# Differential heads' probabilities turned in 32x32 blocks and carried through DRAM, with values eight steps later

## The chip, the cores and the metric

The kernel runs on one core of a Trainium2 chip. The metric is the device time of one execution in microseconds (us), from three runs. The core has TensorE (matrix products, into PSUM), VectorE, ScalarE and GpSimd, and DMA queues issued from SyncE (SP) and GpSimd. In the profile these are PE (and PEld for its weight loads), DVE, ACT, POOL and SP.

## The reference

One transformer layer on 512 rows of width 1024, all in float32: half a SwiGLU feed-forward, a token mixer, half a second SwiGLU feed-forward, and a final RMS norm. The change lies in the mixer. It has four differential heads (numbers 0 to 3 in the kernel) and eight dilated heads, which the kernel handles in pairs as units 4 to 7. Both are called heads below. A differential head has two score maps, m = 0 and 1:

```python
s = einsum('bhmqd,bhmkd->bhmqk', q_blk, k) * scale
s = where(dist >= 0, s + bias, -inf)
p = softmax(s, axis=-1)
a = p[:, :, 0] - lam * p[:, :, 1]
out = einsum('bhqk,bhkd->bhqd', a, v)        # then a norm over the head's 128 columns
```

The map is causal, so with 512 rows in four blocks of 128 the rows of block i have i + 1 blocks of keys: 128, 256, 384 and 512 columns, 1280 in all. The heads' outputs, side by side, are multiplied by `w_out`.

## The kernel before, in words

Products that need more precision than one pass are made of three: both operands are split into a rounded high part and the remainder (names ending in h and l, `mh` and `ml` among them), and `mm3` (L187 to L190) issues high-high, high-low and low-high. ScalarE makes the high parts, VectorE the remainders.

The mixer is one list of TensorE chunks, the projections of queries, keys and values for all heads, and from step 92 the output projection. `step(t)` (L2042) issues chunk t. `put(t, rank, f)` hangs other work on a step: rank under 10 goes before the chunk, in order of rank, and from 10 behind it. The order on TensorE is the order written. The other engines' order is made by the tile framework, which also sets the waits; it gives a tile's buffer to the next tile of the same tag only when everything that reads or writes the old tile is done. Tags `pr0` and `pr1`, the probabilities of map 0 and 1, have two buffers each, and so have the score banks `s` and the banks `t` in PSUM.

A projection chunk is six 512-column matmuls, a head's projection is eight chunks. Head u starts its scores at step s = 41, 49, 57, 65, 73, 81, 88 and 97 for u = 0 to 7.

- Keys and queries (L1596 to L1692). When the projection is done, `casts_k` casts the upper half of the bank (map 0's 64 rows) into k0 and the lower half into k1; `evac_k` has VectorE make the remainders l0 and l1 from the halves (L1645) and has SP copy each half of each tile into its other half (`other_half`, L1639), so that the query's two parts, one above the other, meet the same keys. `casts_q` and `rests_q` do the queries.
- Scores (`score`, L1730): two matmuls for each block of rows i and map m, then VectorE adds the bias, takes the extremum (mx) and writes the row into `pr0` or `pr1`; ScalarE takes the exponential in place. Two steps are given to each block of rows.
- `combine` (L1745): VectorE scales map 1's rows and adds them to map 0's, so `pr0` holds the head's one matrix.
- `turn` (L1869): TensorE transposes the ten 128x128 blocks of that matrix (L1879), at steps s+9 and s+11 (one step apart for head 0), into `t` banks; ScalarE copies them to a tile with tag `tx` (L1881).
- `values` (L1884), step s+13: ten products, two instructions each, of a turned block and a block of values (L1891).
- `squares`, `mean`, `scale`, `finish`, `finish_low` (steps s+14, s+15, s+18, s+20, s+21): the norm. GpSimd takes the power, VectorE scales the output of all four blocks at once out of PSUM (L1915), TensorE transposes it (L1921), ScalarE writes `mh[u]`, VectorE `ml[u]`.

Heads 5 and, in part, 6 already go another way. `flip` (L1761) has VectorE turn 32x32 blocks of 128x640 (L1766), `away` sends the result to a DRAM tile in four DMAs, one for each 32 partitions, in runs of 1280 bytes (L1772), and `back` reads it in one (L1783) so that the blocks themselves are turned too. Their products are `values_moved` (L1797). Head 6's other half is turned by TensorE in `turn_rows` (L1785), head 4 and head 7 by `turn_part`. Heads 4 to 7 share one `tx` tile, made by `turned_tx`.

SP issues in one queue, in the framework's order: weights (L1401), bias strips (L1165), the key copies (L1640), and the DMAs of `away` and `back`.

The output projection (L2020 to L2024) runs over slices k = 0 to 7, one for each head's `mh` and `ml`, and over four blocks of rows; a chunk has two slices of one block of rows.

Of the kernel before, what the change touches and what calls it, by code (L numbers as in the profile page):

```python
# [14 lines left out]
F32 = mybir.dt.float32  # L15
# [3 lines left out]
ALU = mybir.AluOpType  # L19
# [18 lines left out]
DIRECT = (7,)  # L38
MOVED = {5: (0, 1), 6: (1,)}
PAIRED_ROWS = 5  # L40
BACK = {5: 7, 6: 9}
TAKEN = {5: 16, 6: 13}
# [85 lines left out]
def tile_macaron(ctx: ExitStack, tc, xs, xT, wf, wgu1, wst1, wdg1, wqk, wvd, wo, wgu2, wst2,  # L128
# [1055 lines left out]
    def cast(o, a):  # L1184
        A.copy(o, a)

    def rest(o, a, h):
        V.tensor_tensor(o, a, h.bitcast(F32), op=ALU.subtract)
# [407 lines left out]
    def qk_chunks(u):  # L1596
# [26 lines left out]
        def casts_k():  # L1623
            _, _, k0, k1, _, _ = qk[u]
            pk = st["pk"]
            cast(k0[lo, :], pk[lo, :])
            cast(k1[hi, :], pk[hi, :])

# [6 lines left out]
        def evac_k():  # L1635
            q0, q1, k0, k1, l0, l1 = qk[u]
            pk = st["pk"]

            def other_half(t, a, b):  # L1639
                nc.sync.dma_start(t[b, :].bitcast(F32), t[a, :].bitcast(F32))  # L1640

            other_half(k0, lo, hi)
            other_half(k1, hi, lo)
            for a, b, kx, lx in ((lo, hi, k0, l0), (hi, lo, k1, l1)):
                rest(lx[a, :], pk[a, :], kx[a, :])  # L1645
                other_half(lx, a, b)

# [62 lines left out]
    def attention(u, s):  # L1710
        diff, quick, moved = u < 4, u == 7, u in MOVED
        st = {}
        order = (1, 2, 0, 3) if u >= PAIRED_ROWS else range(NQ)

        def row(m, i):
            w = (i + 1) * P
            if u < PAIRED_ROWS:
                return st["pr"][m][:, OFF[i]:OFF[i] + w]
            o = m * 640 + (0, 0, 2 * P, P)[i]
            return st["pr"][i in (1, 2)][:, o:o + w]  # L1720
# [64 lines left out]
        def turn_rows(part):  # L1785

            tx = st["x", 0] = turned_tx()[:, :1280]
            pt = pp.tile([P, S], F32, tag="t", name=f"pt{u}{part[0][0]}{part[0][1]}", bufs=2)
            n = 0
            for m, i in part:  # L1790
                o = m * 640 + (0 if i == 0 else P)
                for k in range(i + 1):
                    T.transpose(pt[:, n + k * P:n + (k + 1) * P], row(m, i)[:, k * P:(k + 1) * P], ident[:])
                A.copy(tx[:, o:o + (i + 1) * P], pt[:, n:n + (i + 1) * P])
                n += (i + 1) * P

        def values_moved():  # L1797
# [20 lines left out]
        def turn_part(m, part):  # L1818
# [9 lines left out]
            if "tx" not in st:  # L1828
                st["tx"] = turned_tx()
                st["used"] = 0  # L1830
            if quick:
# [14 lines left out]
                return  # L1846
            ptb = st["tx"][:, st["used"]:st["used"] + n]
            st["used"] += n
            A.copy(ptb[:, :n], pt[:, :n])
# [19 lines left out]
        def turn(tiles):  # L1869

            if "tx" not in st:
                st["tx"] = tp.tile([P, 12 * HS], F32, tag="tx", name=f"ptx{u}", bufs=1)
            for own in tiles:
# [38 lines left out]
        def scale():  # L1912
            po3, ob = st["po3"], st["ob"]
            V.tensor_tensor(st["f2"], st["f2"], st["y"][:], op=ALU.mult)
            V.tensor_tensor(ob, po3, st["f"][:].to_broadcast([P, NQ, P]), op=ALU.mult)  # L1915

# [33 lines left out]
        if diff:  # L1950

            step, tv = 2 if u else 1, s + 13
            put(tv - 2 - step, 2, turn, ((0, 2), (1,)))
            put(tv - 2, 2, turn, ((3,),))
            put(tv, 1, values)
            e = tv + 1
            put(e, 7, squares)
            put(e + 1, 7, mean)
            put(e + 4, 7, scale)
            put(e + 6, 3, finish)  # L1960
            put(e + 7, 8, finish_low)
        elif quick:
# [8 lines left out]
        elif moved:  # L1971
# [14 lines left out]
        else:  # L1986
            tv = s + 9
            parts = ((0, 0, 4),), ((1, 1, 4),), ((2, 2, 4), (3, 3, 4))
            for j, part in enumerate(parts):
                for m in range(2):  # L1990
                    put(tv + j, 2, turn_part, m, part)
                put(tv + 4, 1, values_part, part)
            put(tv + 5, 3, finish)
            put(tv + 5, 8, finish_low)

# [307 lines left out]
```

## Time and profile before

| | |
|---|---|
| Three runs | 906.12, 906.31, 906.56 us; median 906.31 |
| The profiled execution | 906.15 us, of which 904.4 are its span, from the first to the last instruction |
| Granted TensorE clock, mean | 0.999 |
| ScalarE copies of turned blocks (L1881) | 12 |
| Key copies by SP (L1640) | 28 DMAs of 128 KB |
| DMA in the whole span | 153.05 MB, mean 169 GB/s |

Rows of the profile have the engine, the line of the kernel, the operation, the tile written and the tiles read, the shape (partitions x elements) and a count. In the views in order of time the first two columns are the start in us from the span's start and the length; a bracket at the end has the idle time of the engine ahead of the instruction and what ended it. In the view of one line the three numbers are the shortest, median and longest length in ns. For DMAs the time to landing is that from issue to the last byte's arrival. A row of a DMA queue has the packets, the megabytes and the time of its packets as a share of 16 engines over the window.

### The profile page before, as it was taken

Reading aid. Unit: us, or ns where it says so; the run is one execution under the profiler, and the core shown is the slowest. Engines: PE = TensorE matmul, PEld = TensorE weight load, DVE = VectorE, ACT = ScalarE, POOL = GpSimd, SP = SyncE. Lnnn points to the kernel's source line nnn. Section 1 sums busy time; section 2 is a strip of 40 time slices with the busy share of each in tenths; the row PEclk is TensorE's granted clock in tenths of the full one; section 3 lists DMA queues with packets and bytes.
Section 4 is the critical chain, followed back from the end, with each engine's and each line's share of the span. In section 5 each row is a group of like instructions: output and inputs, shape, how many; then the busy total and the mean of one; then the engine's idle time right before and its main releaser. Section 6 shows DMA issues by size and latency. Waiting matters only on the chain.

```text
span 904.4 us, 15918 instructions
## 1 busy us (share of the span) xinstructions
PE 894.2 (99%) x5640; PEld 803.6 (89%) x5640; DVE 752.0 (83%) x1519; ACT 566.2 (63%) x1192; POOL 118.3 (13%) x148
## 2 busy tenths in 40 slices
PE   9999999999999999999999999999999999999997
PEld 7888998899998889888888768989999889999885
DVE  7698998889888888887887945888888888988985
ACT  7355666466667766757777665656666546666573
POOL 0101202121122110100000000111112112212200
PEclk9999999999999999999999999999999999999999
DMA  7464869677789663624443713475779679779902
GB/s 259 128 164 121 237 180 241 151 198 185 193 220 276 181 194 84 154 89 141 117 134 99 233 59 117 95 185 138 186 180 247 162 178 247 199 188 237 267 13 93
DMA packets 73903, 153.05 MB, mean 169 GB/s; under 512 B 8480, under 2 KB 10528, under 8 KB 73824
## 3 DMA queue, kind: packets, MB, share of 16 engines
q1 hardware_dynamic: 56240, 119.84, 41.2%
q0 software_dynamic: 17584, 32.20, 21.9%
q8 instruction: 44, 0.72, 0.3%
q14 instruction: 35, 0.29, 0.1%
HBM read 144.24 MB, written 4.10 MB: 164 GB/s over the span
## 4 chain that ended last, share of the span: by engine, by line
PE 94%; DVE 2%; DMA 1%; ACT 1%; issue 1%; SPq 0%; POOLq 0%; DVEq 0%; ACTq 0%
PE pt L188 8%; PE pt L189 8%; PE pt L190 8%; PE pua L188 2%; PE pua L190 2%; PE pua L189 2%; PE pq L188 2%; PE pq L189 1%; PE pk L190 1%; PE pq L190 1%; PE pk L189 1%; PE pk L188 1%; PE pwo L190 1%; PE pwo L188 1%; PE pwo L189 1%; PE pga L188 1%
## 5 line engine op out<-in xcount | busy, mean ns | idle before, releaser
L1742 ACT ACTIVATE pr<-pr,mx 128x128 f32<-128x128 f32 (+3 forms) x64 | 35.9, 562 | 28.4 <-DVE mx L1739 27.3
L544 DVE SCALAR_TENSOR_TENSOR x<-pt,x 128x512 f32<-128x512 f32 x50 | 33.2, 687 | 19.8 <-PE pt L190 12.6
L1739 DVE CUSTOM_DVE_ANT_0 pr<-sc,strip 128x128 f32<-128x128 f32 (+3 forms) x64 | 30.6, 486 | 6.8 <-PE sc L1737 6.0
L450 DVE TENSOR_TENSOR w<-s2b,w 128x512 fp32r<-128x512 f32 x38 | 26.0, 685 | 8.0 <-ACT w L446 8.0
L446 ACT CAST w<-raa 128x512 fp32r<-128x512 f32 x34 | 20.9, 622 | 18.6 <-DVE raa L414 10.3
L446 ACT CAST w<-s2b 128x512 fp32r<-128x512 f32 x38 | 23.6, 620 | 6.3 <-DVE s2b L419 6.3
L446 ACT CAST w<-rab 128x512 fp32r<-128x512 f32 x28 | 17.1, 622 | 16.3 <-DVE rab L414 7.5
L188 PE MATMUL pwo<-w,mh 128*128 128x512 f32 x64 | 25.9, 405 | 0.2 <-ACT mh L1929 0.2
L190 PE MATMUL pwo<-w,ml 128*128 128x512 f32 x64 | 25.1, 393 | 0.5 <-DVE ml L1938 0.5
L189 PE MATMUL pwo<-w,mh 128*128 128x512 f32 x64 | 25.0, 390 | 0.0
L450 DVE TENSOR_TENSOR w<-s2a,w 128x512 fp32r<-128x512 f32 x30 | 20.5, 684 | 3.0 <-ACT w L446 2.8
L446 ACT CAST w<-s2a 128x512 fp32r<-128x512 f32 x30 | 18.6, 621 | 6.6 <-DVE s2a L419 5.8
L1736 PE MATMUL sc<-k,q 128*128 128x128 f32 (+3 forms) x64 | 21.9, 343 | 0.8 <-DVE mx L1739 0.8
L450 DVE TENSOR_TENSOR w<-raa,w 128x512 fp32r<-128x512 f32 x34 | 22.6, 683 | 0.0
L189 PE MATMUL pxgb<-ttb,w 128*128 128x256 f32 x80 | 22.5, 281 | 0.0
L221 POOL TENSOR_TENSOR fin<-fin,half 128x1 f32<-128x1 f32 (+1 forms) x7 | 4.0, 568 | 137.3 <-DVE fin L1286 85.7
L389 POOL DMA_DIRECT2D s1bg<-wst_dram x10 | 8.7, 873 | 92.8 <-DVE w L450 38.8
L1737 PE MATMUL sc<-l,q 128*128 128x128 f32 (+3 forms) x64 | 20.4, 320 | 0.0
L189 PE MATMUL pxub<-ttb,w 128*128 128x256 f32 x72 | 20.2, 281 | 0.0
L389 POOL DMA_DIRECT2D s1ag<-wst_dram x8 | 7.1, 888 | 94.8 <-DMA s1ag<-wst_dram 32.9
L1416 DVE TENSOR_TENSOR w<-raw_qk,w 128x512 fp32r<-128x512 f32 x24 | 16.5, 688 | 3.6 <-ACT w L1412 3.5
L221 POOL TENSOR_TENSOR yi<-ss,half 128x4 f32<-128x4 f32 x4 | 4.1, 1015 | 113.0 <-DVE ss L1908 113.0
(1176 smaller groups left out, 3932.2 us busy)
## 6 DMA issues: line engine op xcount, KB each, us to landing
raw_qk<-wqk_dram SPq DMA_DIRECT2D x12, 512.0 KB, 3.5
raw0bg<-wst_dram SPq DMA_DIRECT2D x10, 512.0 KB, 5.4
raw0bu<-wst_dram SPq DMA_DIRECT2D x9, 512.0 KB, 5.7
raw_gua<-wgu_dram SPq DMA_DIRECT2D x8, 512.0 KB, 3.6
raw0ag<-wst_dram SPq DMA_DIRECT2D x8, 512.0 KB, 4.9
strip<-bias_rows SPq DMA_DIRECT2D x16, 256.0 KB, 3.7
raw_wo<-wo_dram SPq DMA_DIRECT2D x8, 512.0 KB, 3.5
raw0au<-wst_dram SPq DMA_DIRECT2D x7, 512.0 KB, 5.9
```

Of the source, the lines that this page charges most:

```text
L188: T.matmul(po, wh, mh, start=first, stop=False, skip_group_check=on)
L189: T.matmul(po, wh, ml, start=False, stop=False, skip_group_check=on)
L190: T.matmul(po, wl, mh, start=False, stop=last, skip_group_check=on)
L389: nc.gpsimd.dma_start(t[:], b, accum_op=ALU.add)
L446: A.copy(made[t][0], source(t))
L450: V.tensor_tensor(l, source(t), h.bitcast(F32), op=ALU.subtract)
L544: V.scalar_tensor_tensor(o, a, f, b, op0=ALU.mult, op1=op1)
L1416: V.tensor_tensor(l[:, c:c + 512], raw[:, c:c + 512], h[:, c:c + 512].bitcast(F32), op=ALU.subtract)
L1736: T.matmul(ps[:, :w], qs[:, qi], ks[:, :w], start=True, stop=False)
L1737: T.matmul(ps[:, :w], qs[:, qi], ls[:, :w], start=False, stop=True)
L1739: V.tensor_tensor_reduce(out=pi, in0=ps[:, :w], in1=st["b"][m][:, w - 1::-1], op0=ALU.add, op1=ALU.min, scale=1.0, scalar=3.0e38, accum_ou ...
L1742: A.activation(pi, pi, AF.Exp, scale=-1.0, bias=st["mx"][:, m, i:i + 1], accum_out=st["ls"][:, m, i:i + 1])
```

## The change

For heads 0 to 3:

- `turn` and `values` are replaced by `diff_flip`, `diff_away`, `diff_back` and `diff_values`. The rows are scored in the order 1, 2, 0, 3 and lie in `pr0` so that rows 1 and 2 fill columns 0 to 639 (group n = 1) and rows 0 and 3 columns 640 to 1279 (group 0). VectorE turns the 32x32 blocks of each group into `pr1` of the same head, whose rows are no longer needed, at step s+8 (group 1) and s+12 (group 0). SP sends each group to a DRAM tile in four DMAs, whose runs in DRAM are 32 floats, and reads it at s+13 and s+17 in one DMA, with runs of 640 floats, into one half of the shared `tx` tile, which heads now use in turn. The products follow at s+21, eight steps later than before, and everything behind them moves with them (head 3's `finish` and `finish_low` by one step less).
- `scale` multiplies by ScalarE, block of rows by block of rows, in place of one VectorE operation, and one step earlier in relation to the products.

For the keys of heads 0 to 6: one cast of all 128 rows into k1 and one remainder into l1, in place of two half ones each. k1 and l1 then hold map 0's keys above map 1's, and SP copies: the upper half into both halves of k0 (and l0), then the lower half over k1's (and l1's) upper half. That is six DMAs in place of four, the last two of which overwrite what the first ones read.

Also: head 4's turning and products come one or two steps later, at fixed places in the shared tile; head 5's first `back` one step later; head 6's `turn_rows` takes the two short rows first and copies them in one operation; the output projection's three chunks of slices 4 and 5 take slice 4 for three blocks of rows first, then slice 5.

```diff
+MOVED_DIFF = (0, 1, 2, 3)
+DIFF_FLIP = (12, 8)
+DIFF_BACK = (17, 13)
+DIFF_TAKEN = 21
+PART_PLACES = {(0, 0): 0, (1, 0): 2560, (0, 1): 512, (1, 1): 896, (0, 2): 1280, (1, 2): 1664}
-BACK = {5: 7, 6: 9}
+BACK = {5: 8, 6: 9}
...
         def casts_k():
-            cast(k0[lo, :], pk[lo, :])
-            cast(k1[hi, :], pk[hi, :])
+            cast(k1[:], pk[:])
...
-            def other_half(t, a, b):
-                nc.sync.dma_start(t[b, :].bitcast(F32), t[a, :].bitcast(F32))
-
-            other_half(k0, lo, hi)
-            other_half(k1, hi, lo)
-            for a, b, kx, lx in ((lo, hi, k0, l0), (hi, lo, k1, l1)):
-                rest(lx[a, :], pk[a, :], kx[a, :])
-                other_half(lx, a, b)
+            rest(l1[:], pk[:], k1[:])
+            for t0, t1 in ((k0, k1), (l0, l1)):
+                for b in (lo, hi):
+                    nc.sync.dma_start(t0[b, :].bitcast(F32), t1[lo, :].bitcast(F32))
+            for t in (k1, l1):
+                nc.sync.dma_start(t[lo, :].bitcast(F32), t[hi, :].bitcast(F32))
...
+            if u in MOVED_DIFF:
+                o = (5 * P, 0, 2 * P, 6 * P)[i]
+                return st["pr"][m][:, o:o + w]
...
+        def diff_flip(n):
+            o = (1 - n) * 640
+            t = st["tr", n] = st["pr"][1][:, o:o + 640]
+            V.transpose(t.rearrange("p (c b j) -> p b c j", c=4, b=5), st["pr"][0][:, o:o + 640])
+
+        def diff_away(n):
+            st["pd", n] = d = dp.tile([32, 20, 4, 32], F32, tag=f"pe{n}", name=f"pe{u}{n}")
+            for r in range(4):
+                nc.sync.dma_start(d[:, :, r, :], st["tr", n][32 * r:32 * r + 32, :].rearrange("p (x a) -> p x a", a=32))
+
+        def diff_back(n):
+            o = u % 2 * 1280 + n * 640
+            st["x", n] = turned_tx()[:, o:o + 640]
+            nc.sync.dma_start(st["x", n], st["pd", n][:].rearrange("j (c b) r a -> c j (b r a)", c=4))
+
+        def diff_values():
+            st["po"] = mm_bank(f"po{u}")
+            st["po3"] = st["po"][:].rearrange("p (i d) -> p i d", i=NQ)
+            fo = (u % 4) * P
+            for i, n, b in ((1, 1, 0), (2, 1, 2), (0, 0, 0), (3, 0, 1)):
+                for k in range(i + 1):
+                    T.matmul(st["po3"][:, i, :], st["x", n][:, (b + k) * P:(b + k + 1) * P], vt[0, k][:, fo:fo + P],
+                             start=k == 0, stop=k == i)
...
-                A.copy(tx[:, o:o + (i + 1) * P], pt[:, n:n + (i + 1) * P])
                 n += (i + 1) * P
+            if len(part) > 1:
+                A.copy(tx.rearrange("p (m e) -> p m e", m=2)[:, :, :P], pt[:, :n].rearrange("p (m q) -> p m q", m=2))
+            else:
+                A.copy(tx[:, o:o + n], pt[:, :n])
...
         def scale():
-            V.tensor_tensor(ob, po3, st["f"][:].to_broadcast([P, NQ, P]), op=ALU.mult)
+            for i in range(NQ):
+                A.activation(ob[:, i, :], po3[:, i, :], AF.Copy, scale=st["f2"][:, i:i + 1])
...
-            step, tv = 2 if u else 1, s + 13
-            put(tv - 2 - step, 2, turn, ((0, 2), (1,)))
-            put(tv - 2, 2, turn, ((3,),))
-            put(tv, 1, values)
+            step, tv = 2 if u else 1, s + (DIFF_TAKEN if u in MOVED_DIFF else 13)
+            if u in MOVED_DIFF:
+                for n in range(2):
+                    put(s + DIFF_FLIP[n], 9.2, diff_flip, n)
+                    put(s + DIFF_FLIP[n], 9.3, diff_away, n)
+                    put(s + DIFF_BACK[n], 2, diff_back, n)
+                put(tv, 1, diff_values)
...
-            put(e + 4, 7, scale)
-            put(e + 6, 3, finish)
-            put(e + 7, 8, finish_low)
+            put(e + 3, 5, scale)
+            put(e + 6 - (u == 3), 3, finish)
+            put(e + 7 - (u == 3), 8 if u < 3 else 1, finish_low)
...
-                for n, part in enumerate((((0, 3),), ((1, 3),), ((0, 0), (1, 0)))):
+                for n, part in enumerate((((0, 0), (1, 0)), ((0, 3),), ((1, 3),))):
...
-        chunks += [lambda kp=kp, tt=tt: wo_mm(0, tt, (2 * kp, 2 * kp + 1)) for tt in range(3)]
+        chunks += [lambda kp=kp, tt=tt: wo_mm(0, tt, (2 * kp, 2 * kp + 1)) for tt in range(3)] if kp < 2 else [
+        lambda part=part: [wo_mm(0, tt, (k,)) for k, tt in part]
+        for part in (((4, 0), (4, 1)), ((4, 2), (5, 0)), ((5, 1), (5, 2)))]
```

More of the change, by code (lines that the diff above doesn't have):

```diff
@@ L1712, in attention @@
         st = {}
-        order = (1, 2, 0, 3) if u >= PAIRED_ROWS else range(NQ)
+        order = (1, 2, 0, 3) if u >= PAIRED_ROWS or u in MOVED_DIFF else range(NQ)
         def row(m, i):
             w = (i + 1) * P
+            if u in MOVED_DIFF:
+                o = (5 * P, 0, 2 * P, 6 * P)[i]
+                return st["pr"][m][:, o:o + w]
             if u < PAIRED_ROWS:
@@ L1829, in turn_part @@
                 st["tx"] = turned_tx()
-                st["used"] = 0
             if quick:
@@ L1846, in turn_part @@
                 return
-            ptb = st["tx"][:, st["used"]:st["used"] + n]
-            st["used"] += n
+            o = PART_PLACES[m, part[0][0]]
+            ptb = st["tx"][:, o:o + n]
             A.copy(ptb[:, :n], pt[:, :n])
@@ L1871, in turn @@
             if "tx" not in st:
-                st["tx"] = tp.tile([P, 12 * HS], F32, tag="tx", name=f"ptx{u}", bufs=1)
+                st["tx"] = turned_tx()[:, u % 2 * 1280:(u % 2 + 1) * 1280]
             for own in tiles:
@@ L1950, in attention @@
         if diff:
-            step, tv = 2 if u else 1, s + 13
-            put(tv - 2 - step, 2, turn, ((0, 2), (1,)))
-            put(tv - 2, 2, turn, ((3,),))
-            put(tv, 1, values)
+            step, tv = 2 if u else 1, s + (DIFF_TAKEN if u in MOVED_DIFF else 13)
[5 more added lines that the diff above has]
+                put(tv, 1, diff_values)
+            else:
+                put(tv - 2 - step, 2, turn, ((0, 2), (1,)))
+                put(tv - 2, 2, turn, ((3,),))
+                put(tv, 1, values)
             e = tv + 1
@@ L1987, in attention @@
             tv = s + 9
+            late = 2 * (u == 4)
             parts = ((0, 0, 4),), ((1, 1, 4),), ((2, 2, 4), (3, 3, 4))
@@ L1990, in attention @@
                 for m in range(2):
[L1991 to L1994, printed above, removed]
+                    put(tv + j + late * (1 + (j == 2)) // 2, 2, turn_part, m, part)
+                put(tv + 4 + late, 1, values_part, part)
+            put(tv + 5 + late, 3, finish)
+            put(tv + 5 + late, 8, finish_low)
     for w in plan:
```

## The prediction

> **What bounds the kernel now.** I read the page first (span, busy time, chain), then the stages by windows, then TensorE's rows in order of time, because a busy share says nothing about what a removed instruction gives back.
>
> ```profile
> span 904.4 us, 15918 instructions
> PE 894.2 (99%) x5640; PEld 803.6 (89%) x5640; DVE 752.0 (83%) x1519; ACT 566.2 (63%) x1192; POOL 118.3 (13%) x148
> ...
> PE 94%; DVE 2%; DMA 1%; ACT 1%; issue 1%; SPq 0%; POOLq 0%; DVEq 0%; ACTq 0%
> ```
>
> ```profile
> 404.00:490.00 86.00, 85.24 (x474) 73.22 (x473) 69.35 (x206) 63.41 (x175) 4.06 (x4) 1.00 0.43 125
> 500.00:510.00 10.00, 9.92 (x48) 8.12 (x47) 9.37 (x32) 6.32 (x19) 0.00 (x0) 1.00 0.69 196
> ```
>
> The chain is TensorE for 94% of the span. The change lies between about 400 and 530 us. In the first window, which holds the differential heads (columns: length, then TensorE, weight load, VectorE, ScalarE and GpSimd busy, granted clock, DMA share, GB/s), TensorE is busy 85.24 of 86 us at full clock and VectorE 69.35, ScalarE 63.41. So TensorE work taken out comes off the end; the other engines matter only if they make it wait. In the second window VectorE is at 9.37 of 10: little can be put there.
>
> **What leaves TensorE: 40 transposes.** Each of the four heads drops ten 128x128 transposes (L1879).
>
> ```profile
> L1879 PE MATMUL pt<-ident,pr x40: 270/272/273, 416.0 to 470.1; 128*128 128x128 f32 x40
> ```
>
> ```profile
> 415.72 0.39 PE L190 MATMUL pk<-xh,w 128*128 128x512 f32 x1
> 415.95 0.82 PE L1879 MATMUL pt<-ident,pr 128*128 128x128 f32 x6
> 416.52 0.36 PE L1736 MATMUL sc<-k,q 128*128 128x256 f32 x1
> ...
> 418.22 0.60 PE L1879 MATMUL pt<-ident,pr 128*128 128x128 f32 x4
> 418.57 0.36 PE L1736 MATMUL sc<-k,q 128*128 128x256 f32 x1
> ```
>
> A duration of 272 ns is not what a transpose costs, since the next starts before it ends. The 512-column matmul at 415.72 holds the line for 0.23 us, though it lasts 0.39. Six transposes hold the line from 415.95 to 416.52 (0.57 us) and four from 418.22 to 418.57 (0.35). Per head 0.92 us, four heads **-3.7 us**. Nothing else leaves TensorE: the 40 value products move eight steps later, so do the transposes in `finish` (seven for head 3).
>
> The Trainium skill, "TensorE: Matmul & The Clock Gate", Part 4 (PE-mode transpose), gives about 275 ns for a transpose in one kernel's context, which agrees with the 272 of the row; by that figure, as an estimate, 40 would give 11 us. The starts in the trace speak against counting it so. It is a rival below.
>
> **The tail.** The output projection now takes slice 4 (mh4, ml4) three times before it needs slice 5, and the two short rows of head 6 get one copy after both transposes.
>
> ```profile
> 515.87 1.31 PE L1808 MATMUL po<-ptx_dilated,v 128*64 128x256 f32 x16 [0.35 <-DMA ptx_dilated<-pd]
> 520.90 0.39 PE L190 MATMUL pwo<-w,ml 128*128 128x512 f32 x1
> 521.50 0.50 PE L188 MATMUL pwo<-w,mh 128*128 128x512 f32 x1 [0.22 <-ACT mh L1929]
> 521.84 0.40 PE L189 MATMUL pwo<-w,mh 128*128 128x512 f32 x1
> 522.70 0.50 PE L190 MATMUL pwo<-w,ml 128*128 128x512 f32 x1 [0.46 <-DVE ml L1938]
> ...
> 525.30 0.27 PE L1793 MATMUL pt<-ident,pr 128*128 128x128 f32 x1
> 525.92 0.33 PE L1793 MATMUL pt<-ident,pr 128*128 128x128 f32 x1 [0.36 <-ACT ptx_dilated L1794]
> ```
>
> Against 0.23 us from start to start, the wait for mh5 costs 0.37 + 0.11 (520.90 to 521.50 to 521.84) and that for ml5 0.63 (521.84 to 522.70): 1.1 us. Slice 5 is now needed six matmuls later, 6 x 0.23 = 1.4 us, and a step's scores besides: more than the 1.1 it was late. **-1.1 us**. The second short transpose starts 0.62 us after the first, where the six above took 0.57/6 = 0.09 each; it waits for the copy of the first out of the same bank, which now comes after both: **-0.5 us**. Late next are head 7's scores, whose exponentials pass through ScalarE; I keep the 1.6 whole and hold a rival for it. The wait at 515.87 for head 5's rows from DRAM I leave as it is: `back` goes one step later, into a stretch that head 3's and head 4's products lengthen. The other row order, the fixed places in the shared tile, and head 4's turning and products up to two steps later move work of the same size: 0.
>
> **What VectorE and ScalarE get.**
>
> ```profile
> L1766 DVE STREAM_TRANSPOSE tr<-pr x6: 793/817/839, 498.0 to 513.9; 128x640 f32<-128x640 f32 x6
> ```
>
> ```profile
> L1915 DVE TENSOR_TENSOR ob<-po,f x4: 691/691/692, 434.6 to 487.6; 128x512 f32<-128x512 f32 x4
> ```
>
> ```profile
> L1188 DVE TENSOR_TENSOR l<-pk,k x14: 682/688/695, 376.9 to 491.3; 64x512 fp32r<-64x512 f32 x14
> ```
>
> ```profile
> L1881 ACT COPY ptx<-pt x12: 377/586/587, 416.6 to 470.5; 128x512 f32<-128x512 f32 x8, 128x256 f32<-128x256 f32 x4
> ```
>
> ```profile
> L1899 ACT ACTIVATE ob<-po,cs x16: 347/359/370, 428.4 to 481.3; 128x128 f32<-128x128 f32 x16
> ```
>
> VectorE gains eight block transposes of 128x640, 8 x 0.82 = 6.5 us, and loses four scalings (2.8) and seven of the fourteen half-height remainders: a 64-row operation takes 0.688 and a 128-row one 0.691 of the same width, so one over all rows costs what one half did (-4.8). Net -1.1 us. ScalarE loses twelve copies (8 x 0.586 + 4 x 0.377 = 6.2) and seven half casts, and gains sixteen 128x128 scalings out of PSUM, priced as the squares (16 x 0.36 = 5.7). Both end with no more than before, beside a TensorE 3.7 us shorter: **0** on the end. If that cover fails it is by place: head 3's ml, one operation of the size of the scaling's 0.69, goes from step 86 to 93, into the window with 9.37 of 10, and would cost TensorE that much. The products of heads 3 and 4, now at steps 86 and 88, give VectorE time just ahead of it.
>
> **What the queues get.** Each head sends two groups of four DMAs to DRAM in runs of 32 floats (128 bytes; 2,560 runs, 0.33 MB a group) and reads each back in one. No row shows 128-byte runs. The nearest are the moved heads' DMAs in 1,280-byte runs.
>
> ```profile
> q1 hardware_dynamic: 843, 1.42, 79.0%
> ```
>
> ```profile
> q1 hardware_dynamic: 260, 0.90, 83.0%
> ```
>
> ```profile
> DMA to landing us min/median/max: 2.1/3.6/5.2
> ```
>
> The first row is the window 498 to 504 with such a group in it: 0.79 x 16 x 6 = 75.8 us of engine time, 53 us per MB in 594 packets per MB. The second, 518 to 522, large rows: 0.83 x 16 x 4 = 53.1 us, 59 per MB in 289 packets. More packets cost nothing more, so by bytes a group takes 0.33 x 55 / 16 = 1.1 us. If each run instead cost as much as a packet of the first row (75.8 / 843 = 90 ns), it would be 2,560 x 0.090 / 16 = 14.4 us. I take twice the price by bytes, 2.3 us, since the rows show no fixed price, though none so short, and keep both ends. The third row is the landing of the 1,280-byte writes.
>
> Load: the four scalings in the row of L1915 start from 434.6 to 487.6, so a head takes 53.0 / 3 = 17.7 us, 16.8 without its transposes. The first window's DMA share of 0.43 is 0.43 x 17.7 = 7.6 us a head; two groups add 4.6 and their two reads, by bytes, 2.2: 14.4 of 16.8. It fits, with little room.
>
> The Trainium skill, "DMA: Bandwidth & Descriptors", speaks against the change: its Specifications ask for 512 bytes for full rate and say that less makes a read-modify-write. Its section on small descriptors adds about three cycles to a 128-byte run's four beats: as an estimate 1.1 x 7/4 = 1.9 us a group. No trace here shows either.
>
> **Where a wait is added.** The turned block lies in the head's own `pr1`. That buffer, one of two, goes to head u+2 only when the second group has landed; until then the last user was `combine`. Behind it VectorE's score reduction of head u+2 (step s+17) would stand, and TensorE's score banks behind that. Tightest is head 0 to 2, steps 53 to 58:
>
> ```profile
> 420.63 0.39 PE L188 MATMUL pq<-xh1m,w 128*128 128x512 f32 x1
> ...
> 422.11 2.47 PE L1891 MATMUL po<-v,ptx 128*128 128x128 f32 x20
> 424.33 0.42 PE L1736 MATMUL sc<-k,q 128*128 128x384 f32 x1
> ...
> 431.36 0.82 PE L1879 MATMUL pt<-ident,pr 128*128 128x128 f32 x6
> 431.94 0.31 PE L1736 MATMUL sc<-k,q 128*128 128x128 f32 x1
> ```
>
> ```profile
> 422.59 1.39 DVE L1621 SCALAR_TENSOR_TENSOR q<-pq,q 64x512 fp32r<-64x512 f32 x2
> ```
>
> From 420.63 to 431.94 are 11.3 us; head 0's product (2.2) moves out and head 1's six transposes (0.6) go: 8.5 are left. The flip stands behind the query remainders: 424.0, or 3.4 us in, less 0.7 for the saved key remainder, plus 0.8: done at 3.5 to 4.2. Four DMAs issue over about 1.4 us, the last lands 2.1 to 5.2 later: 7.0 to 10.8 against 8.5. A wait of -1.5 to +2.3 us, of which TensorE feels what exceeds about one step of projections (1.4 us). For the other heads a product of 2.2 us stays inside: no wait. The key copies add two DMAs that wait for the landing of the first four on SP's queue:
>
> ```profile
> 421.26 1.22 SPq L1640 DMA_DIRECT2D l<-l  x2
> 426.77 0.34 SPq L1401 DMA_DIRECT2D raw_qk<-wqk_dram  x1
> ```
>
> ```profile
> DMA to landing us min/median/max: 2.2/2.2/3.9
> ```
>
> The last l copy then issues at about 422.0 + 2.2 to 3.9, so 424.2 to 425.9, before the weights at 426.77 but up to 1.7 us ahead of the first flip's DMAs. The first score on k1 is the one at 431.94, so the keys themselves are in time. For both I charge **+0.6 us**, between 0 and the 2.3 above.
>
> **Sum.** -3.7 - 1.1 - 0.5 + 0.6 = -4.7. The profiled execution took 906.15 (1.75 around its span), 0.16 below the median 906.31 of the three runs: 906.15 - 4.7 = **901.4 us**. From no change this kernel's measurement can tell 0.2%, 1.8 us.
>
> **Rivals.** (1) *Dear short runs, slower.* The writes' price decides. Engine time per head is 7.6 + 2.2 + 2g for a group of g us; it exceeds 16.8 above g = 3.5 (22 ns a run). From there the queue grows by 2 (g - 3.5) a head, and once four heads of it exceed what the loads have in hand, one of three raw buffers of half a head each or 8.4 us, TensorE waits for weights: g = 4.5, 28 ns a run. At half the packet price, g = 7.2, it is 7.4 a head, 30 in all; less the 8.4 and the 5.3 gained, 906.15 + 16 = 922 us. For: 128 bytes is a tenth of any write in the trace. Against: the two rows that show no price per packet. Chance 0.17. (2) *The tail gives it back.* With the mh5 wait gone, head 7's scores through ScalarE and VectorE, or head 5's rows from DRAM, hold TensorE there: only the transposes remain, less 1 to 2 us of waits on `pr1`: 904. For: 9.37 of 10 at 500 to 510. Chance 0.12. (3) *The work was covered, or a wait replaces it*: 906, chance 0.08. Against: TensorE's starts are gapless around the transposes. (4) *The whole 272 ns counts*: 40 x 0.272 = 10.9 instead of 3.7, 894 us; chance 0.03, the starts deny it.
>
> **How the numbers follow.** The forecast, 900 to 903.5, has 0.60. Range 899.5 to 907: the low end is the sum without the 0.6, with the wait at 515.87 gone (0.35) and the idle time of the first window too (86 - 85.24 = 0.76), 899.7; the high end takes in rivals 2 and 3; left out are 1 and 4, 0.20. Faster by over 0.2% (under 904.5): 0.60 + 0.09 of rival 2 + 0.03 = 0.72; within: 0.03 + 0.08 = 0.11; slower: 0.17.
>
> **What would show it.** Right: L1879 gone and steps of the projection 0.35 to 0.57 us shorter; no wait of mh5 at the output projection; DMA share in the head stage near 0.85; the four writes landing within 6 us. Wrong: VectorE's reduction waiting for `pd`, TensorE for VectorE's mx by more than 1 us a head, or weights waited for.

## The result and the profile after

Slower: 930.21 us (median of 6 runs, 927.63 to 932.35) beside 906.40 us for the kernel before in the same comparison (6 runs, 905.98 to 908.05), a ratio of 1.0259, 95% interval 1.0236 to 1.0282. Forecast were 901.4 us and a range of 899.5 to 907.0. The profiled execution took 932.35 us, and its page answers to the one shown of before:

```profile
span 930.6 us, 15916 instructions
...
PE 900.4 (97%) x5600; PEld 809.1 (87%) x5600; DVE 749.3 (81%) x1516; ACT 559.5 (60%) x1188; POOL 118.2 (13%) x148
...
PE 86%; DMA 6%; DVE 3%; SPq 2%; ACT 1%; issue 1%; POOLq 0%; DVEq 0%; POOL 0%; ACTq 0%
```

TensorE has 40 instructions fewer and is busy 6.2 us longer (900.4 after 894.2). DMA has gone from 1% of the chain to 6%. The two windows of before:

```profile
404.00:490.00 86.00, 69.71 (x329) 58.78 (x328) 57.70 (x170) 44.85 (x128) 2.04 (x2) 0.90 0.67 149
500.00:510.00 10.00, 10.00 (x55) 8.59 (x54) 6.53 (x24) 9.60 (x31) 1.01 (x1) 1.00 0.97 226
```

In the head stage TensorE is busy for 69.71 of 86 us where it was 85.24, at a clock of 0.90; the DMA share is 0.67, not the 0.85 foretold: the 16 engines together are not full. Who waits there, by the waits between 380 and 580 us (total, times, longest):

```profile
DVE pr L1744 <- PE sc L1742: 40.5, 21, 9.5
PEld po L1801 <- DMA ptx_dilated<-pe: 21.1, 4, 9.5
PE po L1801 <- DMA ptx_dilated<-pe: 20.4, 4, 9.3
```

Each of the four heads' products (L1801) waits for its read-back from DRAM, and VectorE then waits for TensorE. SyncE's instructions show one such case, head 0's products, and the chain of waits all four:

```profile
426.62 0.63 SPq L1793 DMA_DIRECT2D ptx_dilated<-pe  x1
427.31 0.43 SPq L1406 DMA_DIRECT2D raw_qk<-wqk_dram  x1
428.19 6.55 SPq L1788 DMA_DIRECT2D pe<-pr  x4
434.85 0.57 SPq L1793 DMA_DIRECT2D ptx_dilated<-pe  x1
```

```profile
434.85 10.42 DMA ptx_dilated<-pe
445.31 2.50 PE po L1801 x10
...
459.76 9.14 DMA ptx_dilated<-pe
...
484.72 7.93 DMA ptx_dilated<-pe
...
500.64 14.79 DMA ptx_dilated<-pe
```

The second group's read-back is issued behind four writes of the next head that take SyncE 6.55 us, and it then needs 10.42 us to land; the others need 8 to 15. TensorE's clock falls in the wait, as the windows around it show:

```profile
434.00:445.00 11.00, 2.04 (x15) 1.69 (x13) 3.71 (x7) 2.32 (x6) 0.00 (x0) 0.80 0.69 134
445.00:452.00 7.00, 6.69 (x24) 5.90 (x25) 1.52 (x6) 0.49 (x2) 0.00 (x0) 0.58 0.45 99
452.00:468.00 16.00, 12.40 (x66) 10.43 (x64) 12.20 (x38) 11.56 (x34) 1.04 (x1) 1.00 0.82 180
```

In the 7 us after the wait the granted clock is 0.58; full clock is back from 452. The Trainium skill, "TensorE: Matmul & The Clock Gate", Part 1, has the clock halved after an idle window of about 3.4 us and full again after as long a busy one; the trace agrees in kind (an idle 9.3 us, then 7 us at 0.58), but the low clock lasts longer here: along the chain, matmuls of 512 columns start 0.43 us apart up to 450.8 us and 0.23 apart from 451.3, some 6 us behind the wait. Behind the second and the third wait, of 4.5 and 4.7 us, the clock is 0.59 (469 to 476 us) and 0.60 (493 to 500).

### The profile page after: what moved, and what is told of

It is laid out like the page before. It is cut to its first block, busy times and chain, and to the rows that moved or that the text cites. A ratio compares the mean times of both kernels' runs of the same rounds, so it can differ in the third digit from the quotient of the medians.

```text
span 930.6 us, 15916 instructions
## 1 busy us (share of the span) xinstructions
PE 900.4 (97%) x5600; PEld 809.1 (87%) x5600; DVE 749.3 (81%) x1516; ACT 559.5 (60%) x1188; POOL 118.2 (13%) x148
## 4 chain that ended last, share of the span: by engine, by line
PE 86%; DMA 6%; DVE 3%; SPq 2%; ACT 1%; issue 1%; POOLq 0%; DVEq 0%; POOL 0%; ACTq 0%
PE pt L195 8%; PE pt L193 8%; PE pt L194 8%; DMA ptx_dilated<-pe 5%; SPq L1788 2%; PE pua L195 2%; PE pua L194 2%; PE pua L193 2%; PE pwo L193 1%; PE pwo L195 1%; PE pwo L194 1%; PE pga L193 1%; PE pga L195 1%; PE pga L194 1%; PE po L1801 1%; PE pygb L193 1%
## 5 line engine op out<-in xcount | busy, mean ns | idle before, releaser
L1747 ACT ACTIVATE pr<-pr,mx 128x256 f32<-128x256 f32 (+3 forms) x64 | 36.0, 562 | 58.6 <-DVE mx L1744 56.7
L1744 DVE CUSTOM_DVE_ANT_0 pr<-sc,strip 128x256 f32<-128x256 f32 (+3 forms) x64 | 30.5, 485 | 40.9 <-PE sc L1742 40.5
L1801 PE MATMUL po<-v,ptx_dilated 128*128 128x128 f32 x80 | 14.9, 353 | 20.4 <-DMA ptx_dilated<-pe 20.4
L1801 PEld LDWEIGHTS po<-v,ptx_dilated 128*128 128x128 f32 x80 | 13.7, 257 | 21.4 <-DMA ptx_dilated<-pe 21.1
L1741 PE MATMUL sc<-k,q 128*128 128x256 f32 (+3 forms) x64 | 22.2, 348 | 0.5 <-DVE mx L1744 0.5
L1742 PE MATMUL sc<-l,q 128*128 128x256 f32 (+3 forms) x64 | 21.0, 330 | 0.0
```

Of the source, the lines that this page charges most:

```text
L1741: T.matmul(ps[:, :w], qs[:, qi], ks[:, :w], start=True, stop=False)
L1742: T.matmul(ps[:, :w], qs[:, qi], ls[:, :w], start=False, stop=True)
L1744: V.tensor_tensor_reduce(out=pi, in0=ps[:, :w], in1=st["b"][m][:, w - 1::-1], op0=ALU.add, op1=ALU.min, scale=1.0, scalar=3.0e38, accum_ou ...
L1747: A.activation(pi, pi, AF.Exp, scale=-1.0, bias=st["mx"][:, m, i:i + 1], accum_out=st["ls"][:, m, i:i + 1])
L1801: T.matmul(st["po3"][:, i, :], st["x", n][:, (b + k) * P:(b + k + 1) * P], vt[0, k][:, fo:fo + P], start=k == 0, stop=k == i)
```

## The experiments

Medians are given with the ratio to the kernel before on the same chip and its 95% interval.

**The change in parts.** My first theory was the forecast's rival of dear short runs; against it stood the new key copies, which wait on SyncE's queue.

Run 1, the change without the moved heads (keys, ScalarE's scaling and the tail stay):

```diff
-MOVED_DIFF = (0, 1, 2, 3)
+MOVED_DIFF = ()
```

> The changed kernel with the differential heads left as they were before (turned by TensorE, values at s+13); keys over all rows with six copies, scaling on ScalarE and the tail's edits stay. If the 128-byte runs are the cause (A), the rest costs nothing and the tail gives its 1.6 us: 904 to 906 us. If the two waiting key copies that hold SP's queue are the cause by themselves (B), at least a third of the 24 us stays: over 914 us.

904.42 us, 0.9982 (0.9972 to 0.9992): the rest of the change costs nothing and gains 1.6 us.

Run 2, each group written and read in runs of 2,560 bytes:

```diff
-d = dp.tile([32, 20, 4, 32], F32, ...)
-    nc.sync.dma_start(d[:, :, r, :], st["tr", n][32 * r:32 * r + 32, :].rearrange("p (x a) -> p x a", a=32))
+d = dp.tile([P, 640], F32, ...)
+    nc.sync.dma_start(d[32 * r:32 * r + 32, :], st["tr", n][32 * r:32 * r + 32, :])
...
-nc.sync.dma_start(st["x", n], st["pd", n][:].rearrange("j (c b) r a -> c j (b r a)", c=4))
+nc.sync.dma_start(st["x", n], st["pd", n][:])
```

> The changed kernel with each group written to DRAM and read back in runs of 2560 bytes, same bytes, same DMAs, same places; the reordering between the 32x32 blocks is left out, so the products take wrongly placed blocks. A (short runs): the waits of the products for the read-back go (20 us of TensorE idle, and the lower clock behind it): 900 to 904 us. B (keys) or C (any round trip through SP's one queue comes late): over 915 us.

904.47 us, 0.9974 (0.9963 to 0.9986). Every wait of the differential heads' products for a read-back is gone (the 2.0 us below is head 5's). Its page, and TensorE's waits between 380 and 580 us:

```profile
span 903.3 us, 15914 instructions
...
PE 889.6 (98%) x5600; PEld 799.2 (88%) x5600; DVE 749.4 (83%) x1516; ACT 560.0 (62%) x1188; POOL 118.3 (13%) x148
```

```profile
PE sc L1741 <- DVE mx L1744: 2.2, 3, 0.9
PE po L1840 <- DMA ptx_dilated<-pd: 2.0, 1, 2.0
```

I took this as proof for the short runs. It was none: the edit changes the read as well as the writes.

Run 3, the change with the keys as before (the diff's two key parts undone):

> The changed kernel with the keys as before: two half casts, two half remainders, four copies, none of which waits for another. A: the key copies only suffer, they land late because they stand behind the short runs; 925 to 931 us. B: SP is no longer held for 23.8 us by copies that wait for copies, the groups and their read-back are issued up to 8 us earlier in each head, and most of the wait goes: under 915 us.

924.68 us, 1.0196 (1.0181 to 1.0212): the keys are a quarter of the loss, though by run 1 they cost nothing alone.

Run 4, the kernel before without the 40 transposes (ScalarE copies the rows unturned):

> The kernel before with the 40 transposes of the differential heads left out: ScalarE copies the rows unturned into the tile that the products read, so the products take unturned blocks. By the starts in the trace 3.7 us come off: 902.7 us. By the busy time, 40 times 272 ns, 10.9 us: 895.5 us. If the work was covered: 906.4 us.

902.26 us, 0.9951 (0.9937 to 0.9966): 4.4 us gained, where the starts gave 3.7 and durations 10.9.

Runs 5 and 6, writes of 640 bytes and a stationary operand with a step of five (run 6 with the old keys as well):

```diff
-V.transpose(t.rearrange("p (c b j) -> p b c j", c=4, b=5), ...)
+V.transpose(t.rearrange("p (c j b) -> p b c j", c=4, b=5), ...)
...
-d = dp.tile([32, 20, 4, 32], F32, ...)
+d = dp.tile([4, 32, 4, 160], F32, ...)
...
-nc.sync.dma_start(st["x", n], st["pd", n][:].rearrange("j (c b) r a -> c j (b r a)", c=4))
+nc.sync.dma_start(st["x", n], st["pd", n][:].rearrange("c j r e -> (c j) (r e)"))
...
-    T.matmul(st["po3"][:, i, :], st["x", n][:, (b + k) * P:(b + k + 1) * P], ...)
+    T.matmul(st["po3"][:, i, :], st["x", n][:, b + k::5], ...)
```

> The changed kernel with the groups sent in runs of 160 floats (640 bytes, five times longer): VectorE writes the turned blocks with the five row blocks innermost, DRAM has the order of the moved heads' tile, and the products read the turned rows with a step of five floats. Same result, same DMAs and places. A (short runs): the waits of the products go, 904 to 907 us, near the run with 2560-byte runs. If 640 bytes are still too short, or the weight loads with a step of five are slow: over 912 us.

> As the run before, with the keys as before (four copies, none of which waits for another). If the key copies cost nothing by themselves, the same time within 1 us. If they hold SP's queue, so that the groups, the bias strips and the read-back come late also with long runs (the run with 2560-byte runs has VectorE waiting 2 us for a strip), 2 to 3 us less: 901 to 904 us.

911.85 us, 1.0048 (1.0033 to 1.0063), and with the old keys 913.83, 1.0071 (1.0056 to 1.0086): the new keys don't cost here. No wait for these read-backs is left. What is left shows in the products' rows of run 5 (busy, mean ns), and behind them in the same rows of run 2:

```profile
L1802 PEld LDWEIGHTS po<-v,ptx_dilated 128*128 128x128 f32 x80 | 18.2, 315 | 0.2
L1802 PE MATMUL po<-v,ptx_dilated 128*128 128x128 f32 x80 | 18.0, 380 | 0.0
```

```profile
L1801 PE MATMUL po<-v,ptx_dilated 128*128 128x128 f32 x80 | 9.6, 275 | 0.0
L1801 PEld LDWEIGHTS po<-v,ptx_dilated 128*128 128x128 f32 x80 | 9.5, 192 | 0.3
```

The 80 products take 18.0 us instead of 9.6: 8.4 us more on TensorE, more than the 5 that the run is slower than the kernel before. With ScalarE laying the read-back in order (run 8b, eight more copies) the products go back to 276 ns, but the copies cost more than they save:

> As the run with the read-back laid in order by ScalarE, but group 1 is read back one step later: there the next head's read-back came into the half of the tile that the head's products still had to read, so that the products waited for it, and the run told nothing of the stationary step. Theory that the run with 640-byte runs lost its 5 us to stationary operands read with a step of five: the 80 products take about 0.12 us from start to start, the waits are gone, and the time is 902 to 905 us. Rival, that carrying the heads through DRAM costs even so, by the slower flip (1.39 us where the plain one takes 0.85 us) and by eight copies of 1.43 us on ScalarE: 908 to 912 us.

```profile
L1796 ACT COPY ptx_dilated<-ptx_dilated 128x640 f32<-128x640 f32 x8 | 11.0, 1372 | 8.6 <-DMA ptx_dilated<-pe 8.6
```

918.51 us, 1.0125 (1.0112 to 1.0139): my theory of this run fell. A first form of it, whose read-back came into a place still in use, took 929.86 us and tells nothing.

**Other queues.** Runs 7 and 7b issue the writes on GpSimd's or ScalarE's queue, run 10 the read-backs on GpSimd's, run 13 these with the old keys:

```diff
-nc.sync.dma_start(d[:, :, r, :], ...)
+nc.gpsimd.dma_start(d[:, :, r, :], ...)     (7; 7b: nc.scalar; 10 and 13: the read-back on nc.gpsimd)
```

> The changed kernel, 128-byte runs, with the writes of the groups issued from GpSimd's queue; everything else stays on SP. If the price of the short runs is that SP stands still while it issues them and that reads and weights stand behind them in SP's rings, the waits of the products go: under 912 us. If it is that the engines or the memory are full with them whoever issues them: 925 us or more.

> The changed kernel, 128-byte runs, with the writes issued from ScalarE's queue. If SP's queue is what is held: under 915 us, with some loss because ScalarE issues 32 DMAs of 0.6 us or more and waits for the flips. If it is the engines or the memory: 925 us or more.

> The changed kernel with its short-run writes on SyncE's queue as they are, but with the read-backs issued by GpSimd's queue, so that no read-back stands behind the next head's writes on SyncE. Theory that the order on SyncE's queue makes the read-back late: TensorE's waits for the read-back fall from some 9 us to under 2 us a head, the time is 906 to 915 us, and what is left are bias strips and weights behind the writes. Rival, that the writes' short packets fill the DMA engines' queues, which every read passes whatever engine issued it: waits of 5 us and more for the read-back stay, and the time is 922 us or more.

> Short-run writes on SyncE's queue and read-backs on GpSimd's, as in the run with the read-backs there (922.2 us), and the keys cast and copied as in the kernel before. Theory that what was left in that run is the six key copies, which land 7 to 10 us after their issue behind the short runs, while scores wait for them: with the old keys, whose copies are asked for earlier and are four of 64 rows each, the time falls to 912 to 917 us. Rival, that late bias strips and weights are what is left: 920 us or more.

Run 7: 914.27 us, 1.0076 (1.0060 to 1.0091). Run 7b: 928.50, 1.0242 (1.0219 to 1.0264). Run 10: 922.21, 1.0169 (1.0153 to 1.0186). Run 13: 915.75, 1.0110 (1.0091 to 1.0129), as its theory had it. No queue removes the loss, but run 7 takes back most of it, and between its theory's 912 and its rival's 925 it decides for neither; "The read" comes back to it. ScalarE's queue only moves the wait to the issuing engine (36.1 us of waits for the writes there, none of the products for a read-back). Run 10 keeps one such wait, 4.8 us, and is slow even so. What run 7b is good for is the price of a run: its queue carries the short writes alone. From the DMA queues of 405 to 500 us (packets, MB, share of 16 engines):

```profile
q10 hardware_dynamic: 20992, 2.62, 16.4%
```

0.164 x 16 x 95 us / 20,992 = 11.9 ns a packet, so 2,560 / 16 x 0.0119 = 1.9 us a group.

Run 12, runs twice as long, the read as in the change:

```diff
-d = dp.tile([32, 20, 4, 32], F32, ...)
+d = dp.tile([32, 10, 4, 64], F32, ...)
...
-nc.sync.dma_start(st["x", n], st["pd", n][:].rearrange("j (c b) r a -> c j (b r a)", c=4))
+nc.sync.dma_start(st["x", n], st["pd", n][:].rearrange("j x r a -> j (x r a)").rearrange("j (c e) -> c j e", c=4))
```

> The changed kernel with each group written to DRAM in 256-byte runs, half as many as in the change, at places where the five blocks of a row part are not brought into their order (that part of the computation is changed; the products read the same number of values from the same tile). Theory that the cost goes with the number of runs, which fill the queues of the DMA engines: half the runs, half of the 25.7 us between short and long runs, 914 to 919 us. Rival, that it is a matter of bounds being overrun (a read-back that is late only from a certain rate): most of the cost is gone already, 905 to 909 us; or, if the price goes with the number of DMAs and not of runs, 925 us or more.

925.00 us, 1.0185 (1.0167 to 1.0204): half the runs, and most of the loss still there.

**The read.** Two things in the traces had been passed over. Among the DMA issues of 410 to 500 us (KB each, median us to landing) the change's read-backs have no landing time:

```profile
ptx_dilated<-pe SPq DMA_DIRECT2D x7, 320.0 KB
...
l<-l SPq DMA_DIRECT2D x12, 128.0 KB, 7.9
```

And among the packets under 512 bytes, where the marks of completion are counted, some are missing. The line of the page for the change, then for run 2:

```profile
DMA packets 97072, 160.14 MB, mean 172 GB/s; under 512 B 29728, under 2 KB 31776, under 8 KB 96992
```

```profile
DMA packets 77712, 160.14 MB, mean 177 GB/s; under 512 B 9344, under 2 KB 11392, under 8 KB 77632
```

Without the 8 x 2,560 short runs the change has 9,248, which is 96 fewer than 9,344, 12 for each of eight read-backs: 4 marks instead of 16. The read's access pattern, `c j (b r a)`, has an outermost dimension of 4, and `j` doesn't merge with it; with all DMAs on SyncE's queue, every kernel in which the waits vanished (runs 2, 5 and 6) read 128 rows in one dimension. Three runs separate the pattern from the data and the writes. Run 14 reads another tile, written once in long runs, 128 rows in a row; run 15 the same old data in the change's pattern; run 16 is the whole change with each read-back as four DMAs of 32 rows:

```diff
-nc.sync.dma_start(st["x", n], st["pd", n][:].rearrange("j (c b) r a -> c j (b r a)", c=4))
+nc.sync.dma_start(st["x", n], kept[0][:])                                (14)
+nc.sync.dma_start(st["x", n], kept[0][:].rearrange("j c e -> c j e"))    (15)
+for c in range(4):                                                       (16)
+    nc.sync.dma_start(st["x", n][32 * c:32 * c + 32, :],
+                      st["pd", n][:].rearrange("j (c b) r a -> c j (b r a)", c=4)[c])
```

> The changed kernel with its short-run writes as they are, but each read-back takes the same 2,560 bytes a partition from another DRAM tile, which the first group wrote once in long runs (the products then don't use their own head's probabilities: that part of the computation is changed). The read-backs keep their places on SyncE's queue behind the writes. Theory that the queue is what holds the read-back (it is served after 1,280 to 5,120 short packets and two key copies on the same queue): the waits stay at 5 us and more a head and the time is 924 us or more. Rival, that the memory is slow to give back what was just written in short runs (in the changed kernel some packets behind the writes last about 1 us): with old data to read the waits fall under 2 us a head and the time is 906 to 914 us.

> As the run whose read-backs take old data from another tile (911.0 us; there the products don't use their own head's probabilities either), but that tile is read in the pattern of the changed kernel: four blocks of 32 rows as the outermost dimension, rows 10,240 bytes apart. The traces leave completion marks of 4 bytes, and the changed kernel has 96 fewer of them than the run with long runs, 12 for each of its eight read-backs: four instead of sixteen. Theory that such a read is cut by its outermost dimension and served by four of the 16 DMA engines, 32 rows each, and that everything behind it waits for these four: the waits for the read-back are back, and the time is 924 us or more, though the data are old. Rival, that the memory is slow to give back what was just written in short runs: 908 to 913 us, as with the other old data.

> The changed kernel, whole, with each read-back issued as four DMAs of 32 rows, one for each block, so that the outermost dimension of each is 32 and no longer 4. Addresses, run lengths, the short-run writes and all else stay. Theory that the spread over four engines is what made the read-back late: the waits for it are gone, completion marks are sixteen a DMA, and the time is 906 to 912 us, what is left being the short-run writes and 24 more issues on SyncE. Rival, that freshly written short runs are slow to read, or that the short runs fill the queues: the waits of 5 to 9 us a head stay and the time is 922 us or more.

Run 14: 911.02 us, 1.0050 (1.0036 to 1.0064). Run 15: 929.21, 1.0250 (1.0230 to 1.0270). Run 16: 915.96, 1.0102 (1.0084 to 1.0120). Old data in the change's pattern are as slow as the change, so freshness is not the cause; fresh data at the same addresses, in DMAs of 32 rows, are hardly waited for (0.4 us in all). The DMA issues of run 14, run 15's wait, then the DMA issues of run 16 and its page:

```profile
ptx_dilated<-kept SPq DMA_DIRECT2D x8, 320.0 KB, 4.7
k<-k SPq DMA_DIRECT2D x15, 128.0 KB, 2.8
l<-l SPq DMA_DIRECT2D x15, 128.0 KB, 2.4
```

```profile
PE po L1804 <- DMA ptx_dilated<-kept: 21.0, 4, 7.8
```

```profile
ptx_dilated<-pe SPq DMA_DIRECT2D x32, 80.0 KB, 2.9
```

```profile
DMA packets 97552, 160.15 MB, mean 175 GB/s; under 512 B 30208, under 2 KB 32256, under 8 KB 97472
```

The 480 marks more than in the change are 32 x 16 less 8 x 4. The Trainium skill, "DMA: Bandwidth & Descriptors", section "Why a DMA increments its semaphore by 16 and not by 1", states the rule: a DMA runs on the largest number of engines up to 16 that divides the size of the slowest dimension on both sides, each marking its own completion; its Rules for kernel authors warn of an outermost dimension under 16. Marks and times agree with it. That the engines are four is inferred from the marks, since the profile doesn't name engines.

Run 7 shows how the read and the writes meet. Its reads have the change's pattern (9,248 packets under 512 bytes, again 96 too few), but its writes go over GpSimd's queue in long packets. Its wait, and its reads in the chain of waits:

```profile
PE po L1801 <- DMA ptx_dilated<-pe: 7.0, 4, 2.8
```

```profile
431.23 8.13 DMA ptx_dilated<-pe
...
447.39 12.19 DMA ptx_dilated<-pe
...
467.72 11.03 DMA ptx_dilated<-pe
...
485.42 12.17 DMA ptx_dilated<-pe
```

Almost without short packets, reads in this pattern still take 8 to 12 us to land. But SyncE asks for them earlier, head 0's second one at 431.23 us instead of 434.85, and TensorE waits for them 7.0 us in all instead of 20.4. So the late landing doesn't need the short writes, and most of the waiting needs both. The read in flight also holds the writes behind it: the four of 428.19 take SyncE 6.55 us in the change and 6.71 in run 15, but 3.46 in run 14.

Run 16 is 4 us above its theory's range. What stays in run 16 and run 14 is the short writes. In run 14 TensorE waits for VectorE, and VectorE for bias strips that were issued behind the writes:

```profile
PEld sc L1741 <- DVE mx L1744: 9.5, 6, 3.1
...
DVE pr L1744 <- DMA strip<-bias_rows: 7.3, 2, 4.7
...
PE sc L1741 <- DVE mx L1744: 7.1, 6, 2.7
```

**The tail.** Run 11 is the kernel before with the output projection's order and head 6's one copy alone; run 9 is run 1 with head 5's read-back and head 4's transposes at their old steps.

```diff
-BACK = {5: 8, 6: 9}
+BACK = {5: 7, 6: 9}
...
-            late = 2 * (u == 4)
+            late = 0 * (u == 4)
```

> The kernel before with two edits of the change alone: the output projection takes heads 4 and 5 apart and in the new order, and head 6's short rows are turned first and copied at once. The prediction's terms for these are 1.1 us and 0.5 us: 904.9 us beside 906.5 us. Rival, that another operand of the output projection is late instead: 906.2 us or more, no difference that can be told.

> The changed kernel with the differential heads not moved (as in the run of the rest alone, 904.4 us), and with head 5's read-back and head 4's transposes at the steps that they had in the kernel before. Theory that the later steps, made to clear the heads' buffers, give back part of the tail's gain by a wait for head 5's read-back (1.6 us there against 0.35 us before): that wait shrinks below 0.5 us and the time is 903.0 to 903.6 us. Rival, that the wait only moves to another operand: 904.4 us again, within 0.4 us.

Run 11: 905.01 us, 0.9980 (0.9971 to 0.9989). Run 9: 903.91, 0.9971 (0.9960 to 0.9983), the fastest kernel of the study that leaves nothing out; the wait of 1.6 us for head 5's rows in run 1 is gone from its trace, though the two intervals overlap. It is the change without its main part.

## Why the prediction was wrong

By ratios, the way from the kernel before to the change is: 2.4 us gained with long runs (run 2), 6.9 lost by the short writes (run 14 against run 2, 0.0076 x 906.5), 18.1 lost by the read's pattern (run 15 against 14, 0.0200), and 0.8 left over, within the noise. The terms must add up, taken in this order, and another order would share them out otherwise: the 18.1 is the pattern's price where short writes stand on the same queue. Run 7, with the same read and the writes elsewhere, is 9.2 us slower than run 2 (1.0076 against 0.9974), with whatever GpSimd's queue costs. No run has the change's read beside long writes on SyncE.

**The step that failed** is in "What the queues get": "two groups add 4.6 and their two reads, by bytes, 2.2". The read was priced as if 16 engines shared it. By its marks it runs on four, with 32 rows of 2,560 bytes on each, and it landed after 8 to 15 us instead of about 4 (2.8 to 6.1 in run 2). No landing of a read stood in the sum at all, and none of the signs of being wrong was a product that waits for its read-back. Behind the reads, weights and l copies were late too: they landed in 8.6 and 7.9 us at the median (4.8 and 2.4 in run 14), and six times SyncE stood until a key copy had landed, 23.8 us in all (3.4 in run 14). This fits the 5.5 us that the keys, free alone, cost by run 3; no run separates it. The page of the Trainium skill that I weighed has the rule, and the diff shows the pattern.

**The clock** was not in the sum either. Against run 2 the span is 27.3 us longer; TensorE is busy 10.8 us more (900.4 to 889.6) for the same instructions, and idle 16.5 more. Most of the first is the lower clock behind the waits: three times 7 us at 0.58 to 0.60 are some 3 us each.

**The rival with the right sign** had another mechanism. It asked for 4.5 us a group; the writes take 1.9, under the 2.3 that I took. What short writes do cost is time on SyncE, where the prediction had 1.4 us for four of them. The issues of the writes (ns min, median, max) in the change, then in run 14, whose reads are in one dimension, then in run 2:

```profile
L1788 SPq DMA_DIRECT2D pe<-pr x32: 577/637/2963, 413.9 to 497.5; - x32
```

```profile
L1788 SPq DMA_DIRECT2D pe<-pr x32: 561/636/1328, 413.9 to 480.0; - x32
```

```profile
L1788 SPq DMA_DIRECT2D pe<-pr x32: 303/422/1285, 413.2 to 474.5; - x32
```

Bias strips stand behind them (the pair asked for at 439.72 us in run 2 is asked for at 442.42 in run 14). Run 14 is 6.9 us slower than run 2, where the sum had 0.6; that late strips are all of it isn't shown. The 0.6 was for `pr1` and the key copies, and among the change's waits none is for that buffer.

**Right:** the 40 transposes (3.7 by starts; 4.4 in run 4, and TensorE is busy 4.6 us less in run 2); the tail's 1.6 (1.8 in run 11, and no wait of mh5 in the trace after); VectorE's and ScalarE's exchange at nothing (the scalings and the keys in run 1; with the flips too, in run 2, VectorE is busy 749.4 us after 752.0 and ScalarE 560.0 after 566.2). The later `back`, left as it was, costs: 2.0 us of wait in run 2 against 0.35 before. With the 2.2 for scores, most of it behind late strips, that is 3.9 us, more than the 2.3 by which the gain with long runs falls short of the 4.7 forecast.

Open: why the rows of one read-back take so long even on four engines, run 7 included. 32 packets of 2,560 bytes, at the 100 to 230 ns that most of that size take in this trace, are 3 to 7 us; whether the rest is other work queued on these four engines the profile doesn't tell, since it doesn't name engines.

## What to carry to other kernels

Look at the outermost dimension of both sides of every DMA before pricing it by bytes: a row order of "4 x 32" that doesn't merge ran on four engines here, by its marks, and cost 18 us beside short writes on the same queue; splitting it into four DMAs of 32 rows gave 14 us back. Price a transfer that something waits for by its landing and by what is queued behind it, not by its share of the engines. And when an experiment changes a layout, both of its sides change: vary one at a time before calling a cause shown.

## What the runs showed of the hardware that I had not expected

- A stationary operand read with a step of five elements loads in 315 ns instead of 192, and its product takes 380 instead of 275 (run 5 against run 2).
- VectorE's 32x32 transpose of 128x640 takes 0.84 us into blocks side by side (run 2) and 1.41 us into a layout with a step of five (run 5).
- GpSimd's queue joins the short runs: 2.62 MB in 1,536 packets in run 7, where ScalarE's took 20,992 in run 7b.
- A wait of 4.5 to 9.3 us leaves TensorE at a mean clock of 0.58 to 0.60 over the next 7 us.
